# A planner that shares one DMA pipe among loads, and gate and up columns taken through the depth together

## The chip, the cores and the metric

The kernel runs on one core of one Trainium2 chip, in one launch. The core has a matrix engine (TensorE, in the profile PE, with its weight loads as PEld), a vector engine (DVE), a scalar engine (ACT), GpSimd (POOL) and a queue engine (SyncE, SP) that issues most of the DMA transfers. The time is in device microseconds (us), from the start of the program to its end on that core; times of several runs are given as a median.

## The reference, cut to what matters

Two layers of a macaron block are computed on a sequence of 512 tokens of width 1024. Each layer is a gated feed-forward network (FFN), a mixing stage (RWKV-7, gated linear attention and attention into a fixed memory, merged by gates) and a second FFN. All arrays are float32.

```
for l in range(DEPTH):                      # DEPTH = 2
    x = x + 0.5 * swiglu_ffn(rmsnorm(x, ffn1_norm[l]), ffn1_w_in[l], ffn1_w_out[l])
    ...                                     # the mixing stage
    x = x + 0.5 * swiglu_ffn(rmsnorm(x, ffn2_norm[l]), ffn2_w_in[l], ffn2_w_out[l])
return rmsnorm(x, final_norm)

def swiglu_ffn(h, w_in, w_out):             # w_in 1024 x 5632, w_out 2816 x 1024
    gate, up = jnp.split(h @ w_in, 2, axis=-1)
    return (jax.nn.silu(gate) * up) @ w_out
```

## The kernel before, in words

**Layout.** The activations lie transposed: eight tiles x[0] to x[7] of 128 channels by 512 tokens. Every large product is made in three reduced-precision matmuls (mm3, L674): an operand is split into a rounded part "hi" (ACT copies it) and a remainder "lo" (DVE subtracts), and hi*hi, hi*lo and lo*hi are added up in PSUM. So every block of weights that arrives by DMA costs one ACT and one DVE instruction before TensorE can use it (weight, L647, in the mixing stage and the output products; piece, L782, in the FFN).

**The FFN** (ffn, L801). norm_in (L699) splits x, scaled by the norm's gain, into xhi and xlo. The factor 1/rms of each token comes separately, from rstd (L733): squares on ACT, sums on DVE, small matmuls into the PSUM tile ps_f (read in the profile as ps_f<-one,sqa and, after a square root on ACT, ps_f<-cst,rt), and a copy rs; it is multiplied in only after a product is in PSUM. The 5632 columns of w_in are taken as 22 pairs of a gate block and an up block of 128 columns each, in two halves of 11; after each half comes the product with half of w_out. A pair is done in one of two ways:

- whole(j) (L814): the pair's weights are four pieces of 128 by 512 (256 KB each), one for each of gate and up and each half of the depth. Stored order: piece 0 is gate with x[0] to x[3], piece 1 up with x[4] to x[7], piece 2 gate with x[4] to x[7], piece 3 up with x[0] to x[3]. The gate is made in a tile ps_b over pieces 0 and 2, then the up in a tile ps_i over pieces 3 and 1: 24 matmuls of 512 columns each.
- begin, middle and end (L843 to L877): seven half-size products instead of eight (a Strassen-Winograd scheme, called Strassen pairs below), on 256 columns. It needs sums of blocks of x (half_sums, L753: four rounds of subtractions on DVE and splits on ACT and DVE) and sums of weight blocks. loads(j) (L829) issues for each pair a tile wa (256 KB), a tile wraw (512 KB) and a tile fs (512 KB) from SP, and an accumulating 512 KB transfer onto fs from POOL, behind which DVE adds up fq.

The first pairs of an FFN's first half are whole ones, which give time to make the half sums: 3 in the first FFN of layer 0, 2 in each of the other three (NWHOLE, L28). There are 79 Strassen pairs in all. Raw weights come through a ring wraw of 3 buffers (load, L666) that all stages share; split weights of the FFN lie in five buffers, three named hi/lo in one pool and two in the FFN's own.

**The order of the work** is not that of the program text. Every engine call is recorded (Recorder, L257), and at build time a planner arranges the calls: run (L401) simulates the five engines as a list scheduler, each taking among its ready calls the most urgent (TensorE mostly the first in program order), with the durations that cost (L323) gives: busy, how long the engine is taken, and took, when the result is there. An engine that is free takes whatever is ready. urgency (L504) then goes backwards through the plan: a matmul is due at the place it has in the order of TensorE, and everything else is due in time for what needs it. plan (L522) repeats this six times and keeps the order with the earliest simulated end. issue (L541) emits the calls in that order; each engine of the chip executes its own in that order, and waits at one whose inputs or buffers are not there. All recorded instructions therefore have L288 in the profile.

For a DMA from SP the planner assumes that the queue is taken for 440 ns and that the data is there 1750 ns plus 3.4 ns for each 1024 bytes later (512 KB: 3.49 us), and 2000 ns more in the FFN; for one from POOL 5500 ns plus the same share. Transfers don't slow each other in it:

```
            size = 4 * some[0].n * (1 if some[0].flat else some[0].rows[1] - some[0].rows[0])
            o.busy, o.took = 440, 1750 + size * 3.4 / 1024 + (2000 if self.part == "ffn" else 0)
```

Of the kernel before, what the change touches and what calls it, by code (L numbers as in the profile page):

```python
# [19 lines left out]
P = 128  # L20
T = 512
D = 1024
KD = 8
# [217 lines left out]
class Op:  # L241
    def __init__(self, n, engine, what, call, deps):
        self.n, self.engine, self.what, self.call = n, engine, what, call
        self.deps, self.kind, self.pool, self.tile = deps, 1, None, None
        self.busy = self.took = self.start = 0.0
        self.mode = self.table = self.takes = None


class Engine:
# [7 lines left out]
class Recorder:  # L257
# [2 lines left out]

    def __init__(self, tc):
        self.tc, self.ops, self.open, self.closed, self.entered, self.kind = tc, [], [], [], [], 0
        self.part = None
        for e in self.ENGINES:
            setattr(self, e, Engine(self, e))

    def op(self, engine, what, call, deps):
        o = Op(len(self.ops), engine, what, call, dict.fromkeys(deps))
        o.kind = self.kind
        self.ops.append(o)  # L270
        return o

# [50 lines left out]
    def cost(self, o, ins, outs, a, k):  # L323

        out = outs[0] if outs else None
        col = any(v.n == 1 and not v.flat for v in ins[1:])
        psum = any(v.psum for v in ins)
        if o.engine == "tensor":
            n = out.n
            wide = ins[0].n > 64  # L330
            if o.what == "transpose":
                o.busy, o.took = 109, 275
            elif ins[0].dt == F32R:
                o.busy = n / 2.4 + 13.7
                o.took = n / 2.4 + 177
            else:
                o.busy = 2 * max(108 if wide else 58, 2 * n / 2.4 + 2.7)
                o.took = o.busy / 2 + 2 * n / 2.4 + 168
            up = lambda q: 32 if q <= 32 else 64 if q <= 64 else 128
            o.mode = (o.what != "transpose" and ins[0].dt == F32R, up(ins[0].rows[1] - ins[0].rows[0]), up(ins[0].n))  # L340
        elif o.engine == "vector":
            n = max(v.n for v in ins + outs)
            if o.what == "reciprocal":
                o.took = 130 + 6.3 * n
            elif o.what == "tensor_tensor_scan":
                o.took = 139 + 2.11 * n
            elif o.what == "memset":
                o.took = 60 + n / 0.96
            else:
                fast = o.what in ("tensor_scalar", "tensor_copy") and not psum  # L350
                o.took = ((n / 2 if fast else n) + 151) / 0.96 + (55 if col and o.what != "tensor_tensor" else 0)
            o.busy = max(o.took - 80, 60)
        elif o.engine == "scalar":
            n = out.n
            o.took = 0.83 * n + (166 if psum else 207) + (90 if col else 0) + (95 if "accum_out" in k else 0)
            o.busy = o.took - 90 + (100 if "accum_out" in k else 0)
            o.table = {AF.Tanh: "exp", AF.Exp: "exp", AF.Sqrt: "sqrt", AF.Ln: "ln", AF.Silu: "silu",
                       AF.Sigmoid: "sig"}.get(a[2])
        elif o.engine == "gpsimd" and o.what == "dma_start":
            o.busy, o.took = 1000, 5500 + 4 * out.n * P * 3.4 / 1024  # L360
        elif o.engine == "gpsimd":
            o.took = 95 + 0.84 * out.n
            o.busy = o.took
        else:
            some = ins + outs
            size = 4 * some[0].n * (1 if some[0].flat else some[0].rows[1] - some[0].rows[0])
            o.busy, o.took = 440, 1750 + size * 3.4 / 1024 + (2000 if self.part == "ffn" else 0)


    HOP, SLACK = 34, 60  # L370
# [30 lines left out]
    def run(self, late):  # L401
# [3 lines left out]
        ready, free = {e: [] for e in self.ENGINES}, dict.fromkeys(self.ENGINES, 0.0)  # L405
        wait = dict.fromkeys(self.ENGINES, None)
        est = dict.fromkeys(self.ops, 0.0)
        events, count, table, last, done = [], 0, None, None, 0
        order, used, held = [], {}, {}

        def key(o):
# [32 lines left out]
        while events:  # L444
            t, _, what, o = heapq.heappop(events)
            touched = set()
            while True:
                if what == "ready":
                    if o.engine is None:
                        o.start = t  # L450
                        order.append(o)
                        free_up(o)
                        if o.tile is not None and o.tile.free:
                            k = o.tile.pool, o.tile.tag
                            used[k] -= 1
                            for q in held.pop(k, ()):
                                put(t + self.lag(o, q), "ready", q)
                    else:
                        heapq.heappush(ready[o.engine], (*key(o), o))
                        touched.add(o.engine)  # L460
                else:
                    touched.add(o)
                if events and events[0][0] <= t:
                    t, _, what, o = heapq.heappop(events)
                else:
                    break
            for e in touched:
                if free[e] > t:
                    continue
                while ready[e]:  # L470
                    if e == "tensor":
                        o = self.choose(ready[e], last, est, t)
                        ready[e].remove(o)
                        heapq.heapify(ready[e])
                        o = o[-1]
                    elif e == "scalar":
                        best = min(ready[e], key=lambda q: q[0] + (2000 if q[-1].table not in (None, table) else 0))
                        ready[e].remove(best)
                        heapq.heapify(ready[e])
                        o = best[-1]  # L480
                    else:
                        o = heapq.heappop(ready[e])[-1]
                    if slot(o):
                        break
                else:
                    continue
                o.start = t
                busy = o.busy
                if e == "tensor":
                    if last is not None and o.mode != last:  # L490
                        busy += 45 if o.mode[1:] == last[1:] else 92
                    last = o.mode
                if e == "scalar" and o.table is not None and o.table != table:
                    table = o.table
                    o.start += 1400
                    busy += 1400
                free[e] = t + busy
                order.append(o)
                put(free[e], "free", e)
                free_up(o)  # L500
# [3 lines left out]
    def urgency(self, order):  # L504

        late, at = {}, 0.0
        for o in order:
            if o.engine == "tensor":
                late[o] = at
                at += o.busy  # L510
        for o in reversed(order):
            t = late.get(o, math.inf)
            for q in o.next:
                g = self.lag(o, q)
                t = min(t, late[q] - (o.busy if g is None else o.took + g))
            late[o] = t
        for o in order:
            if late[o] == math.inf:
                late[o] = at + o.start
        return late  # L520
# [35 lines left out]
class Net:  # L556
# [175 lines left out]

    def rstd(self, xs, n, dim, pool, copy=True):  # L733
        nc = self.nc
        acc = self.sumsq(xs, n, pool)
        nt = n // P
        ps = self.small()
# [5 lines left out]
        ps = self.small()  # L743
        for t in range(nt):
            nc.tensor.matmul(ps[:, t * P:(t + 1) * P], rt[:, t:t + 1].to_broadcast([P, P]), self.c("ident"),
                             start=True, stop=True)
        if not copy:
            return ps[:, :n], rt
        rs = pool.tile([P, n], F32, name="rs", tag="rs", bufs=1)
# [51 lines left out]
    def ffn(self, w_in, w_out, norm, aside=None, last=False):  # L801


        nc, l = self.nc, self.l
        with ExitStack() as ctx:
            pool = self.pool("ffn", 2, ctx)
            xs, rs = self.norm_in(norm, pool)
            nc.part = "ffn"
            ops = None
            for b in range(2):  # L810
# [2 lines left out]

                def whole(j):  # L814
                    src = w_in[b, j]
                    pp = []

                    for c, ps in (((0, 2), self.big()), ((3, 1), self.small("i"))):
                        w = [p for c0 in c for p in self.piece(pool, self.load(src, c0 * T, (c0 + 1) * T))]
                        pp.append(self.product(w, xs, ps))  # L820
                    t = pool.tile([P, T], F32, name="ft", tag="ft")
                    nc.vector.tensor_tensor(t, pp[0], rs, ALU.mult)
                    nc.scalar.activation(t, t, AF.Silu)
# [58 lines left out]
                for i, j in enumerate(js):  # L882
                    t = middle(j, *st)
# [839 lines left out]
```

## Time and profile before

| | |
|---|---|
| time, median of 3 runs | 2687.75 us (2681.72 to 2688.56) |
| the profiled execution | 2686.56 us, span 2684.8 us |
| TensorE matmuls busy | 2626.1 us, 98% of the span |
| DVE, ACT, POOL busy | 1920.6 us (72%), 1413.7 us (53%), 91.5 us (3%) |
| mean granted TensorE clock | 0.992 of full speed |
| DMA traffic | 321.99 MB, mean 120 GB/s |

One execution is profiled, and its times are counted from the start of its span; the time of that execution is 1.8 us longer than its span. The stages follow from the chain of work: first FFN of layer 0 to 367 us, mixing stage to 986, second FFN to 1340, first FFN of layer 1 to 1695, mixing stage to 2318, second FFN to 2670 and the last norm to the end. A busy time sums the instructions of an engine; a row of waits names the engine and tile that waited, what released it, and how long; a row of the chain names what the end of the program hung on at that time.

### The profile page before, as it was taken

To read this page: it belongs to the slowest core of one execution; us is meant where nothing else is said; L and a number is where in the kernel's file an instruction comes from. 1 tells how busy PE (TensorE), PEld (TensorE's weight loads), DVE (VectorE), ACT (ScalarE), POOL (GpSimd) and SP (SyncE) were. 2 spreads that over 40 slices of the span, in tenths; PEclk is the share of its full clock that TensorE was granted. 3 is DMA by queue.
4 is the path that set the end of the run, shared out by engine and by line. 5 is a ranking of instruction groups with operands and counts; after the bars stand their busy time and mean duration, and the time that the engine had idled before them with its cause. 6 is when DMAs were issued, how large, how long until landed. Compare 5 with 4: busy or idle time off the path is not lost.

```text
span 2684.8 us, 43432 instructions
## 1 busy us (share of the span) xinstructions
PE 2626.1 (98%) x16108; PEld 2307.4 (86%) x16108; DVE 1920.6 (72%) x3937; ACT 1413.7 (53%) x2757; POOL 91.5 (3%) x193
## 2 busy tenths in 40 slices
PE   7999999999999989999999999999999999999998
PEld 6989988888888879999889898787888888798996
DVE  7848656778887559668488495676878875695783
ACT  6636547574553346446365364674755543563562
POOL 0000000000000000000000000000000000000000
PEclk9999999999999999999999999999999999999999
DMA  6847442321121356555377473522212223575642
GB/s 186 200 117 173 121 163 79 110 66 56 64 71 61 106 157 160 148 144 134 98 187 172 114 176 115 165 75 92 80 59 66 69 75 103 164 177 131 155 121 86
DMA packets 127879, 321.99 MB, mean 120 GB/s; under 512 B 13330, under 2 KB 27858, under 8 KB 127666
## 3 DMA queue, kind: packets, MB, share of 16 engines
q1 hardware_dynamic: 116288, 277.78, 34.9%
q0 software_dynamic: 11376, 41.42, 8.4%
q8 instruction: 127, 2.08, 0.3%
q14 instruction: 88, 0.70, 0.1%
HBM read 307.10 MB, written 12.06 MB: 119 GB/s over the span
## 4 chain that ended last, share of the span: by engine, by line
PE 86%; DVE 7%; DMA 3%; ACT 2%; issue 1%; SPq 0%; DVEq 0%; ACTq 0%
PE ps_b L288 54%; PE ps_i L288 16%; PE ps_f L288 7%; PE ps_c L288 7%; DMA wraw<-in_ffn_in_dram 2%; PE ps_y L288 2%; DVE wlo L288 1%; DVE Z L288 0%; DMA wz<-in_wz_dram 0%; DVE x L288 0%; DVE A L288 0%; ACT whi L288 0%; DVE MA L288 0%; DVE KB L288 0%; DVE knrm L288 0%
## 5 line engine op out<-in xcount | busy, mean ns | idle before, releaser
L288 ACT ACTIVATE whi<-wraw 128x512 fp32r<-128x512 f32 x522 | 320.8, 615 | 550.1 <-PE ps_b L288 498.9
L288 DVE TENSOR_TENSOR wlo<-wraw,whi 128x512 fp32r<-128x512 f32 (+1 forms) x520 | 347.7, 670 | 326.0 <-ACT whi L288 317.0
L288 PE MATMUL ps_b<-xhi,whi 128*128 128x512 f32 (+1 forms) x880 | 353.0, 402 | 0.1
L288 PE MATMUL ps_b<-xlo,whi 128*128 128x512 f32 (+1 forms) x880 | 351.7, 400 | 0.0
L288 PE MATMUL ps_b<-xhi,wlo 128*128 128x512 f32 x864 | 346.2, 401 | 0.0
L288 PE MATMUL ps_b<-mhi,wlo 128*128 128x512 f32 x704 | 277.5, 394 | 0.0
L288 PE MATMUL ps_b<-mlo,whi 128*128 128x512 f32 x704 | 276.1, 392 | 0.0
L288 PE MATMUL ps_b<-mhi,whi 128*128 128x512 f32 x704 | 273.3, 388 | 0.0
L288 PE MATMUL ps_i<-t,hi 128*128 128x256 f32 x1264 | 232.3, 281 | 0.0
L288 PE MATMUL ps_b<-xhi,hi 128*128 128x256 f32 (+1 forms) x704 | 211.1, 300 | 14.1 <-ACT hi L288 13.8
L288 PE MATMUL ps_b<-xhi,lo 128*128 128x256 f32 (+1 forms) x704 | 210.7, 299 | 0.0
L288 PE MATMUL ps_b<-xlo,hi 128*128 128x256 f32 (+1 forms) x704 | 210.7, 299 | 0.0
L288 PEld LDWEIGHTS ps_i<-t,hi 128*128 128x128 f32 x1264 | 195.1, 190 | 0.0
L288 PEld LDWEIGHTS ps_b<-xlo,whi 128*128 128x128 f32 (+1 forms) x880 | 164.2, 187 | 34.2 <-DVE xlo L288 2.1
L288 PEld LDWEIGHTS ps_b<-xhi,whi 128*128 128x128 f32 (+1 forms) x880 | 164.4, 187 | 32.7 <-ACT xhi L288 1.0
L288 PEld LDWEIGHTS ps_b<-xhi,wlo 128*128 128x128 f32 x864 | 162.7, 188 | 32.3 <-issue 1.4
L288 ACT ACTIVATE hi<-wraw 128x512 fp32r<-128x512 f32 x194 | 121.9, 629 | 116.2 <-PE ps_b L288 72.8
L288 PE MATMUL ps_i<-t,lo 128*128 128x256 f32 x632 | 177.7, 281 | 0.0
L288 DVE TENSOR_TENSOR lo<-wraw,hi 128x512 fp32r<-128x512 f32 x194 | 133.1, 686 | 50.3 <-ACT hi L288 50.2
L288 PEld LDWEIGHTS ps_b<-mlo,whi 128*128 128x128 f32 x704 | 132.2, 188 | 30.5
L288 PEld LDWEIGHTS ps_b<-mhi,whi 128*128 128x128 f32 x704 | 132.2, 188 | 29.2
L288 ACT ACTIVATE hi<-fq 128x512 fp32r<-128x512 f32 x158 | 99.9, 632 | 108.0 <-PE ps_i L288 95.0
(360 smaller groups left out, 6224.5 us busy)
## 6 DMA issues: line engine op xcount, KB each, us to landing
wraw<-in_w_main_dram SPq DMA_DIRECT2D x108, 512.0 KB, 3.3
fs<-in_ffn_in_dram SPq DMA_DIRECT2D x79, 512.0 KB, 5.5
fs<-in_ffn_in_dram POOLq DMA_DIRECT2D x79, 512.0 KB, 7.6
wraw<-in_ffn_in_dram SPq DMA_DIRECT2D x79, 512.0 KB, 4.9
wraw<-in_ffn_out_dram SPq DMA_DIRECT2D x64, 512.0 KB, 3.6
wa<-in_ffn_in_dram SPq DMA_DIRECT2D x79, 256.0 KB, 4.7
wraw<-in_ffn_out_dram SPq DMA_DIRECT2D x64, 192.0 KB, 2.3
wraw<-in_w_branch_dram SPq DMA_DIRECT2D x48, 256.0 KB, 2.6
```

Of the source, the lines that this page charges most:

```text
L288: return getattr(getattr(self.tc.nc, engine), what)(*(f(v) for v in a), **{n: f(v) for n, v in k.items()})
```

## The change

It has four parts, three of them in the planner.

1. **DMA durations.** A transfer has a pipe time: its bytes at 230 per ns from SP (512 KB: 2.28 us), at 190 per ns from POOL (2.76 us). In the simulation all transfers go through one pipe, one after the other: one begins 400 ns after its issue or when the pipe is free, and its data is there 1050 ns (SP) or 2550 ns (POOL) after its pipe time. SP is taken for the pipe time of each of its own transfers, so that it chooses its next one, the most urgent of those that are ready, when the last has gone through. The allowance of 2000 ns in the FFN goes.
2. **Due times.** Going backwards, a load counts with its pipe time and 1450 ns (SP) or 2950 ns (POOL), without the time it stood in line.
3. **The norm's small matmuls** (in rstd) are marked loose: they have no due time of their own from their place in the order of TensorE, only that of what needs their result.
4. **Whole pairs.** The pieces are taken in the order 0, 3, 2, 1: gate and up of the first half of the depth together, matmuls in turn into ps_b and ps_i for each of x[0] to x[3], then both for x[4] to x[7]. The number of loads, splits and matmuls stays.

```diff
--- before.py
+++ after.py
@@ -243,7 +243,7 @@
         self.n, self.engine, self.what, self.call = n, engine, what, call
         self.deps, self.kind, self.pool, self.tile = deps, 1, None, None
         self.busy = self.took = self.start = 0.0
-        self.mode = self.table = self.takes = None
+        self.mode = self.table = self.takes = self.pipe = None
 
 
 class Engine:
@@ -260,13 +260,13 @@
 
     def __init__(self, tc):
         self.tc, self.ops, self.open, self.closed, self.entered, self.kind = tc, [], [], [], [], 0
-        self.part = None
+        self.part, self.loose = None, False
         for e in self.ENGINES:
             setattr(self, e, Engine(self, e))
 
     def op(self, engine, what, call, deps):
         o = Op(len(self.ops), engine, what, call, dict.fromkeys(deps))
-        o.kind = self.kind
+        o.kind, o.loose = self.kind, self.loose
         self.ops.append(o)
         return o
 
@@ -357,14 +357,16 @@
             o.table = {AF.Tanh: "exp", AF.Exp: "exp", AF.Sqrt: "sqrt", AF.Ln: "ln", AF.Silu: "silu",
                        AF.Sigmoid: "sig"}.get(a[2])
         elif o.engine == "gpsimd" and o.what == "dma_start":
-            o.busy, o.took = 1000, 5500 + 4 * out.n * P * 3.4 / 1024
+            o.pipe = 4 * out.n * P / 190
+            o.busy, o.took = 1000, o.pipe + 2950
         elif o.engine == "gpsimd":
             o.took = 95 + 0.84 * out.n
             o.busy = o.took
         else:
             some = ins + outs
             size = 4 * some[0].n * (1 if some[0].flat else some[0].rows[1] - some[0].rows[0])
-            o.busy, o.took = 440, 1750 + size * 3.4 / 1024 + (2000 if self.part == "ffn" else 0)
+            o.pipe = size / 230
+            o.busy, o.took = max(440, o.pipe), o.pipe + 1450
 
 
     HOP, SLACK = 34, 60
@@ -405,7 +407,7 @@
         ready, free = {e: [] for e in self.ENGINES}, dict.fromkeys(self.ENGINES, 0.0)
         wait = dict.fromkeys(self.ENGINES, None)
         est = dict.fromkeys(self.ops, 0.0)
-        events, count, table, last, done = [], 0, None, None, 0
+        events, count, table, last, done, dma = [], 0, None, None, 0, 0.0
         order, used, held = [], {}, {}
 
         def key(o):
@@ -486,6 +488,9 @@
                     continue
                 o.start = t
                 busy = o.busy
+                if o.pipe is not None:
+                    dma = max(t + 400, dma) + o.pipe
+                    o.took = dma - t + (1050 if e == "sync" else 2550)
                 if e == "tensor":
                     if last is not None and o.mode != last:
                         busy += 45 if o.mode[1:] == last[1:] else 92
@@ -506,13 +511,15 @@
         late, at = {}, 0.0
         for o in order:
             if o.engine == "tensor":
-                late[o] = at
+                if not o.loose:
+                    late[o] = at
                 at += o.busy
         for o in reversed(order):
             t = late.get(o, math.inf)
             for q in o.next:
                 g = self.lag(o, q)
-                t = min(t, late[q] - (o.busy if g is None else o.took + g))
+                took = o.took if o.pipe is None else o.pipe + (1450 if o.engine == "sync" else 2950)
+                t = min(t, late[q] - (o.busy if g is None else took + g))
             late[o] = t
         for o in order:
             if late[o] == math.inf:
@@ -732,6 +739,7 @@
 
     def rstd(self, xs, n, dim, pool, copy=True):
         nc = self.nc
+        nc.loose = True
         acc = self.sumsq(xs, n, pool)
         nt = n // P
         ps = self.small()
@@ -744,6 +752,7 @@
         for t in range(nt):
             nc.tensor.matmul(ps[:, t * P:(t + 1) * P], rt[:, t:t + 1].to_broadcast([P, P]), self.c("ident"),
                              start=True, stop=True)
+        nc.loose = False
         if not copy:
             return ps[:, :n], rt
         rs = pool.tile([P, n], F32, name="rs", tag="rs", bufs=1)
@@ -813,11 +822,13 @@
 
                 def whole(j):
                     src = w_in[b, j]
-                    pp = []
-
-                    for c, ps in (((0, 2), self.big()), ((3, 1), self.small("i"))):
-                        w = [p for c0 in c for p in self.piece(pool, self.load(src, c0 * T, (c0 + 1) * T))]
-                        pp.append(self.product(w, xs, ps))
+
+                    pp = self.big(), self.small("i")
+                    for c0, half in (((0, 3), 0), ((2, 1), 4)):
+                        w = [self.piece(pool, self.load(src, c * T, (c + 1) * T)) for c in c0]
+                        for k in range(4):
+                            for ps, part in zip(pp, w):
+                                self.mm3(ps, part[k], xs[half + k], half + k == 0, half + k == KD - 1)
                     t = pool.tile([P, T], F32, name="ft", tag="ft")
                     nc.vector.tensor_tensor(t, pp[0], rs, ALU.mult)
                     nc.scalar.activation(t, t, AF.Silu)
```

## The prediction

> **What bounds the kernel now.** I read the page's head first, then the busy times by stage, the places where TensorE (PE) waited, the chain of work, and at one such place the queue of SP.
>
> ```profile
> span 2684.8 us, 43432 instructions
> PE 2626.1 (98%) x16108; PEld 2307.4 (86%) x16108; DVE 1920.6 (72%) x3937; ACT 1413.7 (53%) x2757; POOL 91.5 (3%) x193
> ```
>
> PE is busy 98% of the span and the change takes no matmul away. So all it can win lies in the 59 us in which PE idles, and in the matmuls that run slowly after an idle time. Where are they? The next view gives busy times of stretches; the column behind POOL is the granted clock, then the share of the DMA engines.
>
> ```profile
> core 0: us, PE busy (x) PEld busy (x) DVE busy (x) ACT busy (x) POOL busy (x), PEclk, DMA share, GB/s
> 10.00:56.00 46.00, 38.72 (x154) 30.93 (x155) 34.30 (x67) 29.83 (x54) 2.73 (x3) 0.89 0.67 195
> 990.00:1020.00 30.00, 22.16 (x99) 18.24 (x98) 20.14 (x43) 19.20 (x35) 2.59 (x3) 0.89 0.74 205
> 1340.00:1380.00 40.00, 33.59 (x161) 28.06 (x161) 29.69 (x59) 25.40 (x48) 2.59 (x3) 0.92 0.70 191
> 2320.00:2350.00 30.00, 25.88 (x112) 21.22 (x111) 22.90 (x48) 22.13 (x41) 2.62 (x3) 0.89 0.76 209
> 80.00:280.00 200.00, 200.00 (x1443) 189.14 (x1443) 149.47 (x279) 107.02 (x203) 12.07 (x14) 1.00 0.66 163
> 1020.00:1050.00 30.00, 30.00 (x255) 30.00 (x255) 29.78 (x58) 19.78 (x40) 2.59 (x3) 1.00 0.68 164
> 380.00:980.00 600.00, 594.85 (x3310) 495.16 (x3310) 436.46 (x1002) 323.62 (x668) 10.07 (x52) 1.00 0.26 83
> 1710.00:2310.00 600.00, 593.14 (x3280) 490.02 (x3280) 439.63 (x1004) 325.11 (x672) 9.85 (x46) 1.00 0.27 84
> ```
>
> The first four are the starts of the four FFNs, where the whole pairs run: PE idles 7.3, 7.8, 6.4 and 4.1 us there, at clocks of 0.89 to 0.92. In the stretch 80 to 280, Strassen pairs and an output product, it idles not at all; in the two mixing stages 5.2 and 6.9 us, over 600 us each. So the four starts are the place. The waits of PE itself, in order of time:
>
> ```profile
> 29.56 0.80 PE L288 MATMUL ps_b<-xhi,hi 128*128 128x512 f32 x1 [7.28 <-ACT hi L288]
> ...
> 40.46 1.05 PE L288 MATMUL ps_f<-cst,rt 128*128 128x128 f32 x8
> ...
> 1007.61 2.07 PE L288 MATMUL ps_f<-cst,rt 128*128 128x128 f32 x8 [7.84 <-DVE rt L288]
> ...
> 1348.80 0.50 PE L288 MATMUL ps_i<-xhi,hi 128*128 128x512 f32 x1 [0.51 <-ACT hi L288]
> 1359.66 2.08 PE L288 MATMUL ps_f<-cst,rt 128*128 128x128 f32 x8 [4.07 <-DVE rt L288]
> 1375.51 0.50 PE L288 MATMUL ps_i<-n,hi 128*128 128x256 f32 x2 [1.83 <-ACT ps_i L288]
> ...
> 2336.62 2.08 PE L288 MATMUL ps_f<-cst,rt 128*128 128x128 f32 x8 [4.12 <-DVE rt L288]
> ```
>
> The releaser named is ACT or the norm's rt, but neither is the cause. The chain of work goes on from them to a load:
>
> ```profile
> 15.53 13.32 DMA wraw<-in_ffn_in_dram
> 29.56 6.53 PE ps_b L288 x16
> 45.24 5.53 PE ps_b L288 x24
> 56.21 1.42 PE ps_b L288 x12
> 990.56 14.19 DMA wraw<-in_ffn_in_dram
> 1009.68 4.54 PE ps_b L288 x16
> 1377.52 2.56 PE ps_b L288 x12
> 2338.70 5.08 PE ps_b L288 x14
> ```
>
> A 256 KB piece of the second whole pair took 13.3 and 14.2 us to land. ACT works in order: its split hi waits for that piece, the square root of the norm stands behind the split, PE behind the square root. Why so long, the queue of SP and the DMA engines in 985 to 1008 us say:
>
> ```profile
> 984.82 0.43 SPq L288 DMA_DIRECT2D fs<-in_ffn_in_dram  x1
> ...
> 987.93 0.79 SPq L288 DMA_DIRECT2D fs<-in_ffn_in_dram  x1
> 988.82 0.69 SPq L288 DMA_DIRECT2D wraw<-in_ffn_in_dram  x1
> ```
> ```profile
> DMA packets 2424, 5.62 MB, mean 244 GB/s; under 512 B 221, under 2 KB 221, under 8 KB 2423
> q1 hardware_dynamic: 1993, 4.04, 60.1%
> q0 software_dynamic: 430, 1.57, 34.3%
> fs<-in_ffn_in_dram POOLq DMA_DIRECT2D x3, 512.0 KB, 10.7
> ```
>
> Between 984.82 and 988.82 SP issued three fs and two wa for the Strassen pairs, 2.1 MB, because the ring wraw was full just then; POOL added three accumulates, 1.57 MB. At 244 GB/s that is (2.1 + 1.57)/0.244 = 15 us of transfers around the urgent piece, and it took 14.2. The plan of before let them go because it counts each as alone.
>
> **The ceiling.** PE's warm pace is 5.53/24 = 0.230 us a matmul of 512 columns. Start 1 (10 to 56 us) loses 7.28 and, in its 16 slow matmuls, 6.53 − 16 × 0.230 = 2.84: 10.1 us. Start 2: 7.84, the norm's matmuls 2.07 instead of 1.05, and 4.54 − 3.69 = 0.85: 9.7. Start 3: 0.51 + 4.07 + 1.83, the norm's 1.03, and 2.56 − 1.42 = 1.14 in the Strassen matmuls after the last wait: 8.6. Start 4: 4.12, 1.03, and 5.08 − 14 × 0.230 = 1.86: 7.0. Together 35.4 us.
>
> **Part by part.**
>
> *One pipe, most urgent first.* SP is still greedy in the plan: with the ring full it takes an fs. But it is then taken for 2.28 us, so that in those 4 us at most 4 × 0.23 = 0.92 MB go ahead instead of 2.1, and perhaps one accumulate, 0.52: 1.44/0.244 = 5.9 us, and 1.1 for the piece. The piece of the chain, issued at 990.56, would be there at 997.6 instead of 1004.75. PE ran dry at 1007.61 − 7.84 = 999.8: 2.2 us are left for the two instructions that split it. It just fits, and the pieces behind it are needed 12 matmuls, 2.8 us, later or more. What is moved back is fs, wa and the accumulates: an fs (5.5 us to landing in the stretch of pairs, row below) and its accumulate (10.7) end some 16 us after an issue at about 991, at 1007; the first Strassen pair started after 1009.68 + 4.54 and 24 more matmuls, at 1019.7, would now start 9.7 sooner, at 1010.0, and needs fs 12 half-size matmuls (1.42 us) later. Hidden, with 4 us over. So the DMA waits go, nearly all 35 us, if nothing else is late.
>
> *What is late next: DVE.* Its work at the starts stays (splits, squares' sums, half sums), in less time. Busy there is 34.3, 20.1, 29.7 and 22.9 us; the stretches would shrink to 35.9, 20.3, 31.4 and 23.0: 96, 99, 95 and 100%. In the steady stretch it is 75%; its fullest one, 1020 to 1050, has 99% without a wait of PE, so nearly full is possible when the order is right. I take 93% as what an in-order plan holds: 36.9, 21.7, 31.9 and 24.6 us, that is 1.0 + 1.4 + 0.5 + 1.6 = 4.5 us given back. Bounds: 0, and at 80% (133.8 us instead of 110.6) 23.
>
> *Clock.* After the wait of only 1.83 us twelve matmuls took 2.56 instead of 1.42 us. I add such a loss, 1.1 to 2.8 us by the slow matmuls counted above, for two of the four starts: 4 us. The Trainium skill, "TensorE: Matmul & The Clock Gate", Part 1: The HAM clock gate, has the gate close only after an idle window of about 3.4 us; by that rule waits so short would cost nothing more, and the sum would be 4 us better. The trace differs here, and I go by it.
>
> *The order 0, 3, 2, 1.* The same loads and matmuls. For the first pair it asks for x[4] to x[7] 12 matmuls (2.8 us) later; for the second it asks for its second piece 2.8 us sooner. Where PE is not waiting neither counts; bounds ±2.8 us at each start, taken as 0, because the two pull against each other.
>
> *Loose norm and due times.* The norm's squares and their sums, which compete with the splits for ACT and DVE, may slide until the PSUM tile of the first pair is needed again, by the first Strassen pair. That helps DVE do the splits first; its gain lies within the 93%. Who waits if they slide too far is that pair, in order on PE.
>
> *The mixing stages* are planned anew too. DMA is busy 26% there, so the pipe changes little; PE's whole idle time is 5.2 + 6.9 us. A new order can win half of it or lose as much: ±6, taken as 0.
>
> Sum: 35.4 − 4.5 − 4 = 27 us. The profiled execution took 2686.56 us (span 2684.8); that gives 2659.6, and 2661 against the median of 2687.75, which lies 1.2 above it.
>
> **Rivals.**
>
> *A: DVE takes the place of the DMA.* At 85% DVE the stretches need 40.4, 23.7, 34.9 and 26.9 us: 15 us over what is hoped, 7 more with clock losses than in my sum: the gain is 13 to 16 us, about 2673. For it: the 95 to 100% above, and the wait at 1375.51, where ACT stood behind DVE. Against: the 99% stretch.
>
> *B: it does not do what it says.* The ring of three still fills, SP still sends a Strassen load first, and POOL's accumulates are issued on another queue. The Trainium skill, "DMA: Bandwidth & Descriptors", Queues, rings and completion order, lets each DMA engine go round-robin over its queues packet by packet, where the new plan has one line. The rows q1 and q0, 60.1 and 34.3% of the same stretch, fit that. As a mechanism: three accumulates beside the piece instead of one cost 1.05/0.244 = 4.3 us more, so that it lands at 1002, 2 us after PE ran dry. With its split and the slow clock behind, 5 to 6 of the 9.7 us stay lost, and 20 of the 35 over the four starts; with DVE's 4.5 the gain is some 8 to 10 us: about 2679.
>
> *C: slower.* Without the 2000 ns the plan has a 512 KB load in the FFN done 2.28 + 1.45 = 3.73 us after an idle pipe. The trace has more:
>
> ```profile
> fs<-in_ffn_in_dram SPq DMA_DIRECT2D x6, 512.0 KB, 5.5
> ```
> ```profile
> DVE fq L288 <- DMA fs<-in_ffn_in_dram: 0.8, 2, 0.4
> ```
>
> If ACT and DVE are then ordered for data that comes 1.8 us later, they block in each of the 79 Strassen pairs, and PE after them. From 27/79 = 0.34 us a pair on the gain is gone; at 0.5 us the time is 2700. Against: in 70 to 300 us the second row is the only wait of DVE for such a load, 0.8 us in all. These loads go out as soon as a buffer is free, far ahead of use, which the new price does not alter.
>
> **Chances.** My forecast (a gain of 18 to 41) 0.58, A 0.19, B 0.14, C 0.09. A change under 0.3% (8 us) is about what a measurement of this kernel cannot tell from none; so faster takes the forecast and A with a sliver of B (0.78), the same takes most of B (0.13), slower C (0.09). The range's lower end is the whole ceiling and the mixing stages' 6 us, 41 together: 2646. Its upper end takes in A and the better half of B: 2683.
>
> **What would show it.** Right: the second whole pair's pieces land within 7 us of issue; PE's waits for rt and hi at the four starts fall from 25.7 us to under 8; the granted clock there is over 0.95, DVE at 90% or more; the Strassen stretches as before. A shows as PE waits on hi or ps_i behind a DVE that is never idle; B as wraw landings of 10 us or more; C as ACT or DVE waits for DMA in the Strassen stretches. I am wrong if the four starts shrink by less than 18 us together, or if the mixing stages move by more than 6.

## The result, and the profile after

The changed kernel takes 2643.35 us (median of 4 runs, 2641.93 to 2646.18) against 2687.61 for the one before: 44.3 us less, a ratio of 0.9841 with a 95% interval of 0.9824 to 0.9858. The forecast was 2661, 26.7 us less, in a range from 2646 up: the direction was right and the gain was larger than the range allowed. The profiled execution took 2644.31 us, 42.25 less than that of before, and the account below is of these two.

The head of the page after: the same 16108 matmuls, 42.3 us less span, and PE idle for 29 us instead of 59.

```profile
span 2642.5 us, 43412 instructions
PE 2613.5 (99%) x16108; PEld 2296.7 (87%) x16108; DVE 1921.7 (73%) x3937; ACT 1415.9 (54%) x2757; POOL 91.8 (3%) x193
```

Where did the time come from? The busy times of the engines between the same events of both traces say it. First before: four rows from the first matmul of an FFN's whole pairs to the first of its output product, then for each mixing stage its beginning, up to the end of the first four products of queries and keys (ps_f<-kT,xq), and the rest up to the w_out product. The columns are those of the prediction's table.

```profile
6.48:135.87 129.39, 121.74 (x833) 112.44 (x833) 108.53 (x207) 83.68 (x159) 9.63 (x11) 0.96 0.75 193
985.78:1109.27 123.49, 115.65 (x869) 110.98 (x868) 107.85 (x208) 80.14 (x151) 10.36 (x12) 0.97 0.74 182
1339.83:1463.95 124.12, 117.71 (x869) 112.18 (x868) 107.33 (x207) 78.14 (x148) 10.35 (x12) 0.97 0.75 185
2318.06:2438.91 120.85, 116.73 (x870) 111.72 (x869) 108.25 (x209) 80.45 (x152) 10.38 (x12) 0.97 0.77 186
...
367.27:407.39 40.12, 38.55 (x213) 31.93 (x212) 31.23 (x54) 26.72 (x47) 0.28 (x6) 0.96 0.55 180
407.39:941.82 534.43, 529.28 (x3009) 442.64 (x3007) 394.92 (x934) 290.77 (x615) 9.79 (x46) 1.00 0.24 76
1694.50:1733.60 39.10, 37.68 (x213) 30.42 (x212) 32.02 (x55) 27.20 (x48) 0.33 (x6) 1.00 0.63 198
1733.60:2274.09 540.49, 533.74 (x3019) 443.47 (x3019) 400.76 (x944) 294.98 (x622) 9.85 (x46) 1.00 0.24 77
```

The same after:

```profile
7.53:125.12 117.59, 117.59 (x832) 110.36 (x833) 107.65 (x206) 82.27 (x156) 9.66 (x11) 1.00 0.83 208
969.10:1084.37 115.27, 114.31 (x870) 109.57 (x869) 106.97 (x207) 79.23 (x149) 10.38 (x12) 1.00 0.82 195
1314.90:1429.75 114.85, 113.92 (x869) 109.42 (x868) 107.18 (x207) 78.69 (x149) 10.38 (x12) 1.00 0.80 198
2281.66:2396.87 115.21, 114.55 (x869) 109.33 (x868) 107.96 (x209) 80.03 (x152) 10.41 (x12) 1.00 0.80 198
...
356.57:393.51 36.94, 36.93 (x214) 30.36 (x213) 31.12 (x54) 27.13 (x48) 0.28 (x6) 1.00 0.59 196
393.51:925.14 531.63, 528.00 (x3007) 442.36 (x3006) 395.25 (x934) 291.62 (x614) 9.97 (x46) 1.00 0.24 77
1660.30:1697.15 36.85, 36.85 (x214) 30.36 (x213) 31.80 (x55) 27.72 (x49) 0.28 (x6) 1.00 0.64 210
1697.15:2237.70 540.55, 536.23 (x3020) 443.23 (x3019) 401.99 (x944) 295.47 (x621) 9.83 (x46) 1.00 0.24 77
```

The four starts are 11.80, 8.22, 9.27 and 5.64 us shorter; the first begins 1.05 us later, so they gave 33.9 us. The granted clock there went from 0.96 or 0.97 to 1.00. The mixing stages gave 6.0 and 2.2 us, of it 3.2 and 2.3 at their beginnings. All else, together, gave 0.2.

What became of the waits at a start? The queue of SP at the second FFN of layer 0 after the change, and the landing of the pieces from 968 to 992 us:

```profile
968.14 0.43 SPq L288 DMA_DIRECT2D fs<-in_ffn_in_dram  x1
970.62 2.90 SPq L288 DMA_DIRECT2D wraw<-in_ffn_in_dram  x3
973.61 0.39 SPq L288 DMA_DIRECT2D fs<-in_ffn_in_dram  x1
```
```profile
wraw<-in_ffn_in_dram SPq DMA_DIRECT2D x4, 256.0 KB, 4.6
```

One fs goes out while the ring is full, not three fs and two wa; then three pieces follow at once. A piece lands 4.6 us after its issue (median), where one took 14.2 us before; at the four starts together no piece of a whole pair takes longer than 7.3 us. What PE waited for in the three later starts, one line or two for each:

```profile
PE ps_c L288 <- ACT hi L288: 0.4, 1, 0.4
```
```profile
PE ps_i L288 <- ACT hi L288: 0.9, 1, 0.9
```
```profile
PE ps_f L288 <- DVE sqa L288: 0.4, 1, 0.4
PE ps_i L288 <- DVE lo L288: 0.2, 1, 0.2
```

That is 1.9 us where 18.4 stood, and none at the first start behind the first matmul. DVE at those three starts, from the first matmul of the whole pairs to the first of a Strassen pair, before, then after, and then after in the 30 us behind the first of them:

```profile
985.78:1019.58 33.80, 25.96 (x114) 21.29 (x113) 23.64 (x48) 22.56 (x40) 2.59 (x3) 0.90 0.75 201
1339.83:1370.68 30.85, 26.27 (x114) 20.94 (x112) 20.37 (x42) 19.19 (x34) 2.59 (x3) 0.94 0.80 222
2318.06:2349.22 31.16, 27.04 (x114) 22.03 (x113) 24.55 (x49) 23.02 (x41) 2.62 (x3) 0.89 0.78 213
```
```profile
969.10:993.17 24.07, 24.07 (x113) 19.74 (x112) 22.84 (x48) 21.16 (x38) 2.59 (x3) 1.00 0.93 245
1314.90:1340.05 25.15, 24.22 (x113) 19.73 (x112) 23.42 (x48) 21.62 (x40) 2.60 (x3) 1.00 0.95 252
2281.66:2306.90 25.24, 24.58 (x113) 19.58 (x112) 23.33 (x48) 22.81 (x42) 2.62 (x3) 1.00 0.85 240
```
```profile
995.00:1025.00 30.00, 29.58 (x249) 29.38 (x249) 29.73 (x57) 20.26 (x40) 2.60 (x3) 1.00 0.83 183
```

DVE is 95, 93 and 92% busy there and 99% behind, and PE hardly waits for it. It does nearly the same work in these stretches as before, at 70, 66 and 79% then; and the 99% behind it had before too (1020 to 1050 us, shown in the prediction).

### The profile page after: what moved, and what is told of

It is laid out like the page before. It is cut to its first block, busy times and chain, and to the rows that moved or that the text cites. A ratio compares the mean times of both kernels' runs of the same rounds, so it can differ in the third digit from the quotient of the medians.

```text
span 2642.5 us, 43412 instructions
## 1 busy us (share of the span) xinstructions
PE 2613.5 (99%) x16108; PEld 2296.7 (87%) x16108; DVE 1921.7 (73%) x3937; ACT 1415.9 (54%) x2757; POOL 91.8 (3%) x193
## 4 chain that ended last, share of the span: by engine, by line
PE 91%; DVE 6%; ACT 1%; DMA 1%; issue 1%; DVEq 0%; SPq 0%; ACTq 0%
PE ps_b L288 58%; PE ps_i L288 17%; PE ps_f L288 8%; PE ps_c L288 7%; PE ps_y L288 2%; DVE wlo L288 1%; DMA wraw<-in_ffn_in_dram 1%; DVE Z L288 0%; DVE x L288 0%; DVE knrm L288 0%; DVE t L288 0%; DVE A L288 0%; DVE MA L288 0%; DVE GR L288 0%; DVE AR L288 0%
## 5 line engine op out<-in xcount | busy, mean ns | idle before, releaser
L288 PEld LDWEIGHTS ps_b<-xlo,whi 128*128 128x128 f32 (+1 forms) x880 | 164.1, 187 | 35.2 <-DVE xlo L288 2.8
L288 PEld LDWEIGHTS ps_b<-mhi,wlo 128*128 128x128 f32 x704 | 132.3, 188 | 27.0
```

What stands on the lines that cost most here:

```text
L288: return getattr(getattr(self.tc.nc, engine), what)(*(f(v) for v in a), **{n: f(v) for n, v in k.items()})
```

## The experiments

The theory after the result: how many bytes SP lets out ahead of an urgent piece is what counts, and the new plan's sharing of the DMA engines decides that. Its rivals: the loose norm (PE stood at rt), the order of the pieces, or the shorter landing times. Each kernel ran beside the one before, whose median was 2686.7 to 2687.9 each time.

**The order of pieces alone**: the kernel before with the new whole(j).

```diff
-    for c, ps in (((0, 2), self.big()), ((3, 1), self.small("i"))):
...
+    for c0, half in (((0, 3), 0), ((2, 1), 4)):
```

> The kernel before with the new order of pieces (0, 3, 2, 1) alone; costs, line and due times of before. Theory line (loads that are priced as sharing the DMA engines carry the gain): the second pair's pieces still stand behind the Strassen loads, PE still waits 20 us or more at the four FFN starts, and the time is 2680 to 2692. Rival columns (the order lets PE go on while a piece or the last x tiles are missing): 10 us or more of the 44 come from here, 2678 or less.

2690.54 us, ratio 1.0013 (1.0004 to 1.0023). PE's longest waits are those of before (there 16.6 us for rt and 13.8 for hi):

```profile
PE ps_f L288 <- DVE rt L288: 17.1, 4, 7.0
PE ps_b L288 <- ACT hi L288: 15.3, 2, 8.7
```

**The loose norm alone**: the kernel before with the marks in rstd and the condition in urgency.

```diff
-                late[o] = at
+                if not o.loose:
+                    late[o] = at
```

> The kernel before with the norm's matmuls loose, and nothing else. Theory line: PE no longer stands at rt but at the split hi of the same late piece; waits of 20 us or more stay, 2678 to 2690. Rival norm (PE stood 16 us behind the norm's rt, in its own order, and would have had other work): three starts lose 4 us or more each less, 2674 or less.

2692.68 us, ratio 1.0022 (1.0012 to 1.0032), slightly slower than both theories had it. Half of the waits for rt became waits for the sums before it (sqa); the late piece stayed late:

```profile
PE ps_b L288 <- ACT hi L288: 15.0, 2, 8.5
PE ps_f L288 <- DVE sqa L288: 12.2, 2, 6.5
PE ps_f L288 <- DVE rt L288: 8.7, 3, 7.9
```

So PE stood at rt because ACT stood at the piece; freed of its place, the norm only moved the wait. Why the kernel became some 5 us slower is not shown.

**The DMA part alone**: the changed kernel without the loose norm and with the old order of pieces, that is the hunks of cost, run and the due times of loads.

```diff
-                if not o.loose:
-                    late[o] = at
+                late[o] = at
...
-    for c0, half in (((0, 3), 0), ((2, 1), 4)):
+    for c, ps in (((0, 2), self.big()), ((3, 1), self.small("i"))):
```

> The kernel before with the new DMA durations, the one line and the due times of loads; norm and order of pieces as before. Theory line: it carries nearly all, 2643 to 2652, and the waits of the mixing stages' beginnings go too. Rivals norm and columns: a third or more of the 44 us is missing, 2658 or more.

2645.58 us, ratio 0.9847 (0.9831 to 0.9862). It carries the change.

**Without the new order of pieces**: the changed kernel with the old whole(j).

```diff
-    for c0, half in (((0, 3), 0), ((2, 1), 4)):
...
+    for c, ps in (((0, 2), self.big()), ((3, 1), self.small("i"))):
```

> The changed kernel with the old order of pieces (gate through the whole depth, then up). Theory line: within 4 us of the changed kernel, 2640 to 2648. Rival columns: 10 us or more slower than it, with waits of PE for hi or xhi at the FFN starts.

2642.99 us, ratio 0.9836 (0.9821 to 0.9852): the order of the pieces gives nothing that can be told, alone or beside the rest.

Which piece of the DMA part? It has two that hold transfers back in the plan.

**Without SP's spacing**: the line stays, SP is taken for 440 ns.

```diff
-            o.busy, o.took = max(440, o.pipe), o.pipe + 1450
+            o.busy, o.took = 440, o.pipe + 1450
```

> The changed kernel, but SP is taken for 440 ns by each of its transfers in the plan, as before; the one line stays. Theory throttle (my prediction's step: SP, taken for the pipe time, lets only what fits through go ahead of an urgent piece): the Strassen loads go out in a bunch again whenever the ring is full, and 15 us or more of the 44 are lost, 2658 or more. Rival price (knowing that the line is long is enough, because a load's due time and the planned arrival then order the other engines): 2652 or less.

2659.04 us, ratio 0.9893 (0.9878 to 0.9908): 15.7 us of the 44 lost, the low end of what the theory had. And the loss lies in one place. From the first whole matmul to the output product the first FFN takes 131.9 us (117.6 with the change), the three others 116.1, 113.7 and 114.6. Its queue of SP and its chain show the old picture, three fs and three wa and a piece behind them that lands after 17 us:

```profile
8.99 0.38 SPq L288 DMA_DIRECT2D fs<-in_ffn_in_dram  x1
...
12.35 0.33 SPq L288 DMA_DIRECT2D wa<-in_ffn_in_dram  x1
```
```profile
14.07 17.05 DMA wraw<-in_ffn_in_dram
```

At the other three starts the line alone did as well, but not by letting fewer bytes go ahead. At the second FFN SP still sends two fs and two wa (984.46 to 987.54 us) before the two urgent pieces, and these land 8.8 us after their issue (median of the two). ACT does other work in the meantime and stands only 0.27 us at the split of the first:

```profile
wraw<-in_ffn_in_dram SPq DMA_DIRECT2D x2, 256.0 KB, 8.8
```
```profile
996.22 0.63 ACT L288 ACTIVATE hi<-wraw 128x512 fp32r<-128x512 f32 x1 [0.27 <-DMA wraw<-in_ffn_in_dram]
```

There the rival's reason holds: the plan knows that the piece comes late and puts squares, half sums and their splits before it.

**Without the line**: SP keeps its spacing, but transfers don't wait for one another.

```diff
-                    dma = max(t + 400, dma) + o.pipe
+                    dma = t + 400 + o.pipe
```

> The changed kernel, but transfers don't wait for one another in the plan (each lands its pipe time and 1450 or 2950 ns after its issue); SP is still taken for the pipe time of its own. Theory throttle: SP's own spacing does it, only POOL's accumulates go unseen: within 6 us of the changed kernel, 2640 to 2649. Rival price: 2658 or more.

2644.9 us, ratio 0.9841 (0.9826 to 0.9856): the whole change. So there are two ways to it: the spacing makes the piece land sooner, the line fills the time until it lands.

**Without both**: the two edits above together.

> The changed kernel without the line and with SP taken for 440 ns: what stays are the new landing times of a transfer alone (512 KB in 3.73 us instead of 5.49 in the FFN), the due times, the loose norm and the order of pieces. Theory (line and spacing each hold back the Strassen loads, and one of them must be there): the waits of before come back, 2675 or more. Rival prices: 2665 or less.

2689.75 us, ratio 1.0011 (1.0002 to 1.0019), with waits like those of before:

```profile
PE ps_i L288 <- ACT hi L288: 11.2, 2, 6.5
PE ps_f L288 <- DVE sqa L288: 10.7, 3, 6.1
PE ps_b L288 <- ACT hi L288: 8.1, 2, 7.8
```

At the second FFN the two pieces land about as late as with the line alone, but ACT stands idle at the split:

```profile
wraw<-in_ffn_in_dram SPq DMA_DIRECT2D x2, 256.0 KB, 9.4
```
```profile
997.48 0.63 ACT L288 ACTIVATE hi<-wraw 128x512 fp32r<-128x512 f32 x1 [5.53 <-DMA wraw<-in_ffn_in_dram]
```

New prices, due times, loose norm and order of pieces, without anything that holds a transfer back in the plan, give nothing.

**The spacing alone**: the kernel before with one number changed.

```diff
-            o.busy, o.took = 440, 1750 + size * 3.4 / 1024 + ...
+            o.busy, o.took = max(440, size / 230), 1750 + size * 3.4 / 1024 + ...
```

> The kernel before with one number of its plan changed: SP is taken by each of its transfers for bytes/230 ns instead of 440 ns. No line, no new landing times, no loose norm, old order of pieces. Theory spacing (what matters is how many bytes SP lets out ahead of an urgent piece, and its own spacing says that): it gives nearly the whole change, 2642 to 2652. Rival prices and line (the landing times by which the other engines are ordered are needed too): 2658 or more.

2644.04 us, ratio 0.9843 (0.9829 to 0.9856). One line of code gives what the whole change gives. At the second FFN one fs goes out ahead of the first piece, a wa and an fs before the next, and the pieces land in 5.6 us (median); the landing times and due times in its plan are those of before. PE's longest waits in it, the first of them the beginning of the program:

```profile
PE ps_b L288 <- ACT xhi L288: 8.7, 1, 8.7
PE ps_i L288 <- DVE A L288: 2.4, 5, 0.5
```

**Is DVE full?** The prediction gave back 4.5 us to it. Two kernels do the 16 subtractions of half_sums twice and three times over, with the same values; nothing else is changed.

```diff
+            for _ in range(2):
                 nc.vector.tensor_tensor(t[:, 0, :], b11, b12, ALU.subtract)
                 ...
```

> The changed kernel with the 16 subtractions of the half sums done twice (the same values written again): some 5.5 us more DVE work at each FFN start, 22 us in all, no other change. Theory DVE full (it is 94 to 95% busy at the starts now, so that nothing more fits): most of it shows, 15 us or more slower than the changed kernel, 2658 or more, with PE waits behind DVE. Rival slack (work that is not due at once moves into the Strassen pairs, where DVE is about 90% busy): 6 us or less slower.

> The changed kernel with the 16 subtractions of the half sums done three times: some 8 us more DVE work at each start than in the changed kernel, by the 16 us that the doubled ones added over all. About 94% of 26 us and 8 us more do not fit in the start. Theory spill (what is not due moves into the Strassen pairs behind, where DVE is idle 9% of 90 us, 8 us): 8 us or less slower than the changed kernel, 2651 or less. Theory DVE full: PE waits show, 15 us or more slower, 2658 or more.

Twice: 2646.66 us, 0.9846 (0.9831 to 0.9861), 3.3 us above the changed kernel, with intervals that overlap nearly whole: slack, as the rival had it. DVE was busy 1937.7 us, 16.0 more, so the added work was 4.0 us a start and not the 5.5 that I had expected. Nearly all of it slid behind the start, or pushed other work there: up to the first Strassen pair DVE is busy no more than 0.2 us longer at the three later starts (0.8 at the first), and no stretch is longer. The second FFN's:

```profile
969.33:993.32 23.99, 23.99 (x113) 19.81 (x112) 23.05 (x53) 19.66 (x34) 1.77 (x3) 1.00 0.92 237
```

Three times: 2666.21 us, 0.9926 (0.9912 to 0.9939), 22.9 us above, as the theory of a full DVE had it. DVE was busy 1958.8 us, 9.3 more a start. So between 4.0 and 9.3 us more work a start lies the point at which DVE takes over. There PE waits behind DVE's remainders, in the Strassen pairs just behind the start, and DVE is never idle for 25 us, of which these are the last three rows:

```profile
PE ps_f L288 <- DVE lo L288: 6.8, 3, 2.6
```
```profile
2320.00:2325.00 5.00, 4.00 (x24) 3.34 (x23) 5.00 (x13) 3.61 (x6) 0.87 (x1) 1.00 0.74 194
2325.00:2330.00 5.00, 2.07 (x11) 1.59 (x9) 5.00 (x14) 3.13 (x7) 0.00 (x0) 0.82 0.39 77
2330.00:2335.00 5.00, 4.58 (x20) 4.06 (x19) 5.00 (x11) 1.59 (x4) 0.00 (x0) 0.50 0.16 54
```

**The allowance back** (rival C of the prediction): 2000 ns more for SP's loads in the FFN, behind the line.

```diff
-                    o.took = dma - t + (1050 if e == "sync" else 2550)
+                    o.took = dma - t + ((3050 if o.ffn else 1050) if e == "sync" else 2550)
```

> The changed kernel with 2000 ns added again to the landing of SP's loads in the FFN, behind the one line. My rival C (loads priced too short block the engines in the Strassen pairs) would have this faster by 4 us or more, 2639 or less; the theory that loads go out when a buffer comes free, far ahead of use, has it the same, 2641 to 2647.

2640.89 us (2640.56 to 2645.4), ratio 0.9831 (0.9815 to 0.9847). The median lies 2.5 us under that of the changed kernel and just outside what I had for "the same", but the two ratios' intervals overlap nearly whole: whether it is faster is not settled.

**A whole pair less** in the first FFN of each layer, as a try at a faster version.

```diff
-NWHOLE = [[3, 2], [2, 2]]
+NWHOLE = [[2, 2], [1, 2]]
```

> The changed kernel with one whole pair less, a Strassen pair in its place, in the first FFN of each layer (2 and 1 instead of 3 and 2). A whole pair takes 48 x 0.230 = 11.0 us of PE, a Strassen pair 10.0. If DVE has slack to spare at the starts, 2 us faster than the changed kernel: 2640 to 2643. If the start of a single whole pair, 11 us, is too short for the half sums (some 11 us of DVE) beside the splits, PE waits there and it is 4 us or more slower: 2647 or more.

2644.7 us, ratio 0.9845 (0.9831 to 0.9858): nothing gained, and neither expectation held for both FFNs. By the stretch from the first whole matmul to the output product, that of layer 0 is 1.2 us shorter than with the change (116.4 against 117.6) and that of layer 1, with a single whole pair left, 3.2 us longer (118.0 against 114.8).

## Why the prediction was right in place and direction and wrong in size

- **The place and its cause: right.** PE's time lay at the four FFN starts, behind a 256 KB piece that stood in line with Strassen loads. The ceiling of 35.4 us was met to 33.9. Start by start the ceiling was off by 0.7 to 1.5 us either way. The pieces land in 4.6 us at the second FFN and in 7.3 at most (forecast under 7), the waits fell from 25.7 to 1.9 us (under 8), the clock is 1.00 (over 0.95).
- **"I take 93% as what an in-order plan holds", and the clock loss behind such waits: the step that failed first.** It gave back 4.5 us to DVE and 4 to slow clocks; the starts lost 1.5 us of the ceiling in all, and with the clock at 1.00 none of it to slow clocks. The share was about right: DVE is 92 to 95% busy up to the first Strassen pair. Its price was wrong. I asked all the DVE work of the old stretch to fit into 93% of the new one, or PE to wait. But DVE did nearly that work, at the third start more (22.8, 23.4 and 23.3 us at the three later starts, against 23.6, 20.4 and 24.6 before) with no more than 0.9 us of PE waits at a start. What is not due there can slide into the Strassen pairs behind; the doubled half sums show that 4 us more a start still did so, and the tripled ones that DVE was the next bound after all.
- **"The mixing stages ... ±6, taken as 0": wrong, 8.2 us.** This is the larger part of the miss: the two profiled executions differ by 15.3 us more than the 27 forecast, and of these some 7 come from the step above and 8.2 from here. It is also where the range was too narrow: the starts stayed under their ceiling, the mixing stages went beyond their ±6, which the prediction had named as a sign of being wrong. I took DMA at 26% of 600 us to mean that the pipe changes little. At the beginnings of the two stages DMA is at 55 and 63%, and PE waited there (1.6 us of the first 40, 1.4 of the first 39) at a clock of 0.96 in layer 0. The chain of before had, at both beginnings, a load for a later use; an ACT instruction waited for it with the split of the next weights behind:

```profile
367.42 6.10 DMA wz<-in_wz_dram
...
1694.64 5.76 DMA wz<-in_wz_dram
```

  As at the FFN starts ACT, in its order, stood at a load that landed later than planned (6.1 us where the plan's formula gives 2.2). After the change PE does not wait there, and the two beginnings are worth 5.4 of the 8.2 us. Up to the start of the products named above, each of them takes 35.2 to 36.7 us in every kernel with the spacing or the line, and 37.4 to 42.6 in those with neither. The other 2.8 lie in the rest of the stage of layer 0, where PE idles 3.6 us instead of 5.2. That they have the same cause is not shown; what the runs show is that this whole stage takes 568.5 to 570.9 us in each kernel with the spacing or the line, and 573.0 to 575.3 in those with neither.
- **"Loose norm ... its gain lies within the 93%" and the order of pieces "taken as 0": right.** Neither gives anything, and alone they cost 5 and 3 us.
- **How many bytes go ahead:** 0.92 MB in the 4 us, I had worked out, and the queue after shows one fs, 0.52 MB. SP's spacing was named as what does it; that the line would do it alone too, at three of four starts and without fewer bytes ahead, I had not seen.
- **Rival A** (DVE) begins at 4.0 to 9.3 us more work a start than there is. **Rival B** (nothing held back) is the kernel without line and spacing, 2689.75, and at the first start the one with the line alone. **Rival C** (loads priced too short) did not come: the Strassen pairs of a second half take 108.2 us (187.9 to 296.1) as before (198.6 to 306.8), and with the allowance back the median differs by 2.5 us, which is not settled.

## What to carry to other kernels

Where an in-order queue feeds several users, look for the piece that landed late, and count the bytes issued ahead of it in the few us before: a scheduler that takes transfers as free lets out everything that has a buffer. One price is enough here, the time for which the issuing queue is taken, set to bytes over bandwidth (230 per ns, the one value that was tried); line, prices and due times add nothing to it that can be told. A plan that only knows that the piece will be late can do as well where other work can go before it, as at three of the four starts; at the first, where pieces took up to 17 us, it could not. When a bound on the next engine is worked out, count only what is due in the shortened stretch, and look at every stage's first us by itself: a mean of 26% hid two places at 55 and 63%.

## What the runs showed of the hardware

PE's granted clock fell to half at waits of less than 3 us. In the kernel with tripled half sums this is the longest wait at the last start:

```profile
2328.79 0.58 PE L288 MATMUL ps_f<-n,lo 128*128 128x256 f32 x1 [2.60 <-DVE lo L288]
```

With it, PE is busy 2.07 of the 5 us from 2325. The granted clock is 0.82 over these 5 us, which is half clock for the last 1.8 of them, from about 2328.2 us and so before the wait had ended; in the 5 us behind, where PE is busy 4.58, it is 0.50. "TensorE: Matmul & The Clock Gate" of the Trainium skill (Part 1: The HAM clock gate) has the gate close after an idle window of about 3.4 us; no single wait was that long here, nor was the one of 1.83 us in the kernel before. How much idle time in pieces is enough, these runs do not show.
